# HGRN2 values for four heads in one matmul group, and the HGRN2 norm factor applied in the output stage

## The chip, the cores and the metric

One core of a Trainium2 chip runs the whole program. Five engines work side by side, each through its own instructions in order: TensorE (PE; its weight loads are the row PEld), VectorE (DVE), ScalarE (ACT), GpSimd (POOL) and SyncE (SP), which here mostly issues DMAs. The metric is the device time of one execution in microseconds (us), smaller is better. A change of 0.2% (3.8 us) is about what a measurement of this kernel can tell from no change.

## The reference, cut to what matters

A decoder layer on x of 2048 tokens by 1024 columns, in float32: h = RMSNorm(x), one input projection, two mixers side by side, one output projection, a residual and a last RMSNorm. The change concerns the HGRN2 mixer, eight heads of 128 keys and 128 values each:

```python
def hgrn2_mix(q_raw, f_raw, i_raw, g_raw, lb, norm_w):
    q = silu(q_raw); f = lb + (1 - lb) * sigmoid(f_raw); k = (1 - lb) * sigmoid(-f_raw)
    v = i_raw
    # per head, in chunks: S_t = diag(f_t) S_{t-1} + k_t v_t^T ;  o_t = S_t^T q_t
    ...
    o = o * lax.rsqrt(jnp.mean(o * o, axis=-1, keepdims=True) + EPS)   # over the 128 values
    o = o * norm_w
    o = o.reshape(B_, L, HG_WIDTH) * silu(g_raw)
    return o
```

The norm factor is one number for each token and head. The Mamba-2 mixer, which the change touches little, has such a factor for each token and group (two groups). Then `x = x + concat(hg_out, m2_out) @ w_out`.

## The kernel before

**Tiling.** Tokens go in 4 blocks of 512 (`TB`), each of 4 windows of 128 (`NW`). Activations lie as [channel, token]. Every operand of a projection is split into a high and a low part (`wh`, `wl` for weights, `hh`, `hl` for the normed input; `hr`, `lr` are those of block 0 before its norm factor is known), and a product is three matmul passes, wh·hh, wl·hh, wh·hl, over 8 slices of 128 input columns (`proj`, L345): 24 matmuls of 512 moving columns for 128 output columns. In block 0 the weights are split on ACT, DVE and POOL and saved to DRAM; blocks 1 to 3 read the two parts back.

**Units.** A block runs eight head units `H` (`hg_unit`, L608), eight Mamba units `M` (`m2_unit`, L476), two `B` units (`bc_unit`), one `dt_unit`, and the values `VV`. Each unit has projection steps (three of an `H`, two of an `M`) and later stages (`m0` to `m7` of a head), which are planned so many steps after the unit's start (`DUES`, L35) and run between the projection steps of later units (`plan`, `step`, `flush`, L828 to L839). `block_jobs` (L862) writes out the order of units. Each engine runs in that order, with small shifts by the scheduler.

**Values.** `v_step` (L582) makes v as [token, value] for a pair of heads: the stationary operand is a window of hh or hl, the moving operand 256 columns of weights, and two windows share a PSUM bank. There are two steps for a pair, four pairs a block.

**A head's end.** `m6` (L797) makes the result `po` as [token, value] (stationary att and qa, moving v and the states), squares it on ACT, sums on DVE (L808), makes the factor on POOL (L810) and multiplies on DVE (L812). `m7` (L816) transposes it back on PE (tile `oT`, four transposes), multiplies by the norm weight and the gate (L820) and stores it in DRAM (`mix_d`).

**Mamba norm.** The factors of a group are gathered in `rstg`, transposed and stored once for two blocks (`rg_store`, L853, tile `rgt`). The output stage reads them back broadcast to 128 partitions (`rgb`, L980) and multiplies (L985).

**Output stage.** For each block of tokens `mix_get` (L968) loads two of the 16 mixer tiles (`mr`), splits them into `mh` on ACT (L989) and `ml` on DVE or POOL (L990); `out_mm` (L994) runs three passes of matmuls into one PSUM bank for each of 8 output slices d. `wo_get` (L954) splits the output weights into `woh` on ACT (L959) and `wol` on DVE (L960). The first block starts early: for e = 0 to 8 (`NE` = 9) and the five d of `early` it runs between the last stages of block 3 (`early_step`, L1011); afterwards come e = 9 to 15 for those d, then all 16 e for the other three d, for which the mixes are loaded and split a second time. The tiles `mh`, `ml` share four buffers with the first two output weights, which stay, so two pairs are in flight.

**Memory.** Pools hold work tiles: slots of 512 (tag "s", 19), 1024 (tag "b", 7) and 768 elements; PSUM has 2 banks for projections (`pj`) and 6 for the rest (`px`). The pool `o1` of the output stage takes the place of `hh` and `hl`; a tile in it waits until the tile that lay there has been read for the last time.

## Time and profile before

| | us |
|---|---|
| median of 3 runs (1924.34 to 1927.28) | 1924.44 |
| the profiled execution | 1923.41 |
| its span | 1921.7 |
| PE busy in the span | 1886.1 (98%) |
| DVE busy | 1207.5 (63%) |
| ACT busy | 687.5 (36%) |
| POOL busy | 316.7 (16%) |
| mean granted TensorE clock, share of full speed | 0.996 |

The profiled execution took 1.7 us more than its span and 1.0 us less than the median. Busy shares are over the whole span. A matmul's listed duration reaches past the start of the next one, since they are pipelined, so what a matmul costs in a stream is the distance from its start to the next start. Rows in brackets name a group further below.

### The profile page before, as it was taken

The page shows a single profiled execution, that of the slowest core. Times are in us where ns is not written, and L with a number is a line of the kernel's source. Part 1 is how long each engine was busy: PE and PEld are TensorE (multiplying, and loading weights), DVE is VectorE, ACT ScalarE, POOL GpSimd, SP SyncE. Part 2 cuts the span into 40 slices and gives each one's busy share as a digit, 9 for nine tenths or more (in the row PEclk, how much of TensorE's full clock was granted, in tenths as well). Part 3 has the DMA queues.
Part 4 walks back from the last instruction along what each step waited for, and adds up shares of the span by engine and source line. Part 5 has one row for each costly group of instructions (what it writes and reads, how often), then busy time and mean ns, then how long its engine had stood idle before and what let it go on. Part 6 is the DMA issues. An engine that isn't in the chain of part 4 may idle for free. (4 is left out here: it accounts for less than half of the span.)

```text
span 1921.7 us, 35105 instructions
## 1 busy us (share of the span) xinstructions
PE 1886.1 (98%) x14056; PEld 1599.3 (83%) x14056; DVE 1207.5 (63%) x2904; ACT 687.5 (36%) x1156; POOL 316.7 (16%) x445
## 2 busy tenths in 40 slices
PE   7999999999999999999999999999999999999998
PEld 5788888788888888888888888888888877888898
DVE  8777788865666576655665866556655675424342
ACT  4554454433433343233333333323332433121211
POOL 4312242312011221110112211101110120000000
PEclk9999999999999999999999999999999999999999
DMA  8767777745555566355555554645554454414032
GB/s 266 253 229 262 260 258 250 252 171 175 175 187 189 184 198 192 128 187 174 178 199 176 206 168 137 194 165 167 171 171 164 152 192 170 159 50 148 28 111 88
DMA packets 110899, 344.97 MB, mean 180 GB/s; under 512 B 12224, under 2 KB 21008, under 8 KB 110352
## 3 DMA queue, kind: packets, MB, share of 16 engines
q1 hardware_dynamic: 109536, 341.46, 52.7%
q8 instruction: 111, 1.82, 0.4%
q0 software_dynamic: 96, 0.03, 0.4%
q10 hardware_dynamic: 1104, 1.24, 0.2%
q14 instruction: 52, 0.43, 0.1%
HBM read 262.82 MB, written 79.86 MB: 178 GB/s over the span
## 5 line engine op out<-in xcount | busy, mean ns | idle before, releaser
L999 PE MATMUL po<-mh,woh 128*128 128x512 f32 (+1 forms) x640 | 223.1, 352 | 2.1 <-ACT woh L959 2.1
L999 PE MATMUL po<-mh,wol 128*128 128x512 f32 (+1 forms) x640 | 222.6, 348 | 0.0
L999 PE MATMUL po<-ml,woh 128*128 128x512 f32 (+1 forms) x640 | 221.6, 348 | 0.0
L999 PEld LDWEIGHTS po<-mh,woh 128*128 128x128 f32 x640 | 121.4, 190 | 19.3 <-ACT woh L959 2.9
L999 PEld LDWEIGHTS po<-mh,wol 128*128 128x128 f32 x640 | 121.5, 190 | 16.0 <-issue 0.7
L999 PEld LDWEIGHTS po<-ml,woh 128*128 128x128 f32 x640 | 121.2, 190 | 15.1
L989 ACT CAST mh<-mr 128x1024 fp32r<-128x1024 f32 (+1 forms) x48 | 43.4, 907 | 190.1 <-PE po L999 156.5
L990 DVE TENSOR_TENSOR ml<-mr,mh 128x1024 fp32r<-128x1024 f32 (+1 forms) x46 | 47.5, 1032 | 88.7 <-ACT mh L989 88.4
L122 POOL TENSOR_SCALAR hr<-hss 128x4 f32<-128x4 f32 x32 | 8.3, 259 | 514.5 <-DVE hss L808 514.4
L511 DVE TENSOR_SCALAR csb<-csb,cs 128x128 f32<-128x128 f32 x256 | 66.8, 328 | 31.9 <-ACT ecs L508 31.9
L440 DVE SCALAR_TENSOR_TENSOR xs<-u_x,sm,xs 128x512 f32<-128x512 f32 x96 | 71.8, 748 | 4.2 <-ACT xs L438 3.6
L596 PE MATMUL pv<-wh,hh 128*128 128x256 f32 x480 | 70.2, 289 | 0.0
L596 PE MATMUL pv<-wl,hh 128*128 128x256 f32 x480 | 69.0, 285 | 0.0
L109 POOL TENSOR_TENSOR wl<-wr,wh 128x1024 fp32r<-128x1024 f32 x22 | 55.4, 2523 | 78.5 <-ACT wh L108 63.6
L353 PE MATMUL px<-hh,wh 128*128 128x512 f32 x256 | 67.6, 406 | 0.0
L353 PE MATMUL pz<-hh,wh 128*128 128x512 f32 x256 | 67.5, 405 | 0.0
L596 PE MATMUL pv<-wh,hl 128*128 128x256 f32 x480 | 67.3, 283 | 0.0
L353 PE MATMUL pf<-hh,wh 128*128 128x512 f32 x248 | 65.8, 405 | 0.0
L353 PE MATMUL pq<-hh,wh 128*128 128x512 f32 x248 | 65.2, 405 | 0.0
L353 PE MATMUL pg<-hh,wh 128*128 128x512 f32 x248 | 65.0, 404 | 0.0
L442 POOL TENSOR_TENSOR xs<-xs,u_x 128x512 f32<-128x512 f32 x32 | 41.9, 1310 | 133.8 <-ACT u_x L441 133.8
L353 PE MATMUL pz<-hh,wl 128*128 128x512 f32 x256 | 63.5, 390 | 0.0
(334 smaller groups left out, 4522.9 us busy)
## 6 DMA issues: line engine op xcount, KB each, us to landing
wh<-whd SPq DMA_DIRECT2D x156, 512.0 KB, 4.4
wl<-wld SPq DMA_DIRECT2D x156, 512.0 KB, 3.4
whd<-wh SPq DMA_DIRECT2D x52, 512.0 KB, 5.2
wld<-wl SPq DMA_DIRECT2D x52, 512.0 KB, 4.1
wr<-wt SPq DMA_DIRECT2D x51, 512.0 KB, 5.4
csb<-csd SPq DMA_DIRECT2D x32, 512.0 KB, 5.8
mr<-mixd SPq DMA_DIRECT2D x64, 256.0 KB, 2.9
mixd<-sg SPq DMA_DIRECT2D x32, 256.0 KB, 3.7
```

The lines of the kernel that those rows point to most:

```text
L109: (G if i in (1, 2) or c >= 32 else V).tensor_tensor(lo[:, z], raw[:, z], hi[:, z].bitcast(F32), op=ALU.subtract)
L122: G.tensor_scalar(r, ss, 1.0 / n, EPS, ALU.mult, ALU.add)
L353: state["mm"] = T.matmul(ps, lhsT=a[:, k, :], rhs=b[:, k, :], start=(n == 0), stop=(n == 23))
L440: V.scalar_tensor_tensor(dst, u[:, j:j + TB], cw[:, c, j:j + 1], dst, op0=ALU.mult, op1=ALU.add)
L442: G.tensor_tensor(dst, dst, u[:, 3:], op=ALU.mult)
L511: V.tensor_scalar(csb[:, i, w, :], csb[:, i, w, :], dts["cs"][:, w, h0 + i:h0 + i + 1], 0.0, ALU.subtract, ALU.min)
L596: T.matmul(ps[:, 256 * j:256 * j + 256], lhsT=a[:, k, w * P:(w + 1) * P], rhs=rhs, start=(n == 0), stop=(n == 23))
L989: A.copy(mh[:, :, 0:n], mr[:, :, 0:n])
L990: lo.tensor_tensor(ml[:, :, 0:n], mr[:, :, 0:n], mh[:, :, 0:n].bitcast(F32), op=ALU.subtract)
L999: T.matmul(pss[d], lhsT=a[:, d, :], rhs=b, start=(e == 0 and n == 0), stop=(e == 15 and n == 2))
```

## The change

Three things change together.

1. `v_step` makes the values of four heads at once. The moving operand is 512 weight columns. One step now takes a quarter of the input columns (two slices of 128) for all four windows, whose sums stay open in four PSUM banks (two of `pj`, two of `px`) over four steps. There are two groups of four steps a block instead of four groups of two, so `block_jobs` has the first group at the block's start and the second after M(3). The host lays out the weights to fit.
2. `m6` swaps the operands: stationary v and states, moving att and qa. The result comes out as [value, token], so the transposes go, and the gate and norm weight are applied straight from PSUM. The sum of squares now runs across partitions: `m7` is four matmuls with `ones` (tile `hss`, by `ss_cols`), a copy and the POOL pair, into a tile `nst` that holds the factors of all ten norms of a block.
3. `rg_store` runs in every block and stores 40 rows. In the output stage, `mix_get` reads for each head (e below 8) the broadcast factor (`rgb`, three buffers in `o1`, tile `rgh`) and multiplies `mr` by it on DVE before the split; for the last two half blocks the Mamba factors are read for each half.

Sizes follow: 17 slots "s" and 8 "b", `NE` = 8.

```diff
-    def v_step(tb, pr, i, ws, rec):
+    def v_step(tb, q, j, ws, rec):
...
-            for j in range(2):
-                w = 2 * i + j
+            if j == 0:
+                pjt = lambda w: pj.tile([P, TB], F32, tag="pj", name=f"pv{q}_{tb}_{w}")
+                pxt = lambda w: bank(f"pv{q}_{tb}_{w}")
+                rec["ps"] = [pjt(0), pxt(1), pxt(2), pjt(3)]
+                rec[tb] = [slot("b", [2, 4, P], f"v{q}{z}_{tb}") for z in range(2)]
+            for w in range(NW):
+                ps = rec["ps"][w]
                 n = 0
                 for a, b in ((hh, 0), (hh, 1), (hl, 0)):
-                    for k in range(KT):
-                        rhs = wv[k // 4][b].rearrange("p k c -> p (k c)")[:, (k % 4) * 256:(k % 4) * 256 + 256]
-                        T.matmul(ps[:, 256 * j:256 * j + 256], lhsT=a[:, k, w * P:(w + 1) * P], rhs=rhs,
-                                 start=(n == 0), stop=(n == 23))
+                    for k in range(2):
+                        rhs = wv[b].rearrange("p k c -> p (k c)")[:, k * TB:(k + 1) * TB]
+                        T.matmul(ps, lhsT=a[:, 2 * j + k, w * P:(w + 1) * P], rhs=rhs,
+                                 start=(j == 0 and n == 0), stop=(j == 3 and n == 5))
...
-                T.matmul(po[:, sl], lhsT=att[:, w, :], rhs=v[:, w, :], start=True, stop=False)
-                T.matmul(po[:, sl], lhsT=qa[:, sl], rhs=prevs[w], start=False, stop=True)
-            on = slot("s", [TB], f"on{nm}")
+                T.matmul(po[:, sl], lhsT=v[w], rhs=att[:, w, :], start=True, stop=False)
+                T.matmul(po[:, sl], lhsT=prevs[w], rhs=qa[:, sl], start=False, stop=True)
+            r["on"] = on = slot("s", [TB], f"on{nm}")
+            A.activation(on, po, AF.Square)
+            sg = r["sg"]
+            V.scalar_tensor_tensor(sg, po, hgn[:, hd:hd + 1], sg, op0=ALU.mult, op1=ALU.mult)
+            nc.sync.dma_start(mix_d[hd][tb], sg)
+            advance(hgS[:, hd, :], NW - 1)
+
+        def m7():
+            ssv = ss_cols(r["on"], bank(f"hss{nm}"))
             ss = mp.tile([P, NW], F32, tag="hss", bufs=2, name=f"hss{nm}")
-            A.activation(on, po, AF.Square)
-            V.tensor_reduce(ss, on.rearrange("p (w e) -> p w e", w=NW), axis=AX.X, op=ALU.add)
-            rr = mp.tile([P, NW], F32, tag="hr", bufs=2, name=f"hr{nm}")
-            rstd_cols(rr, ss, P)
...
-        def m7():
-            sg = r["sg"]
-            poT = bank(f"oT{nm}")
-            transpose4(poT, r["on"])
-            V.scalar_tensor_tensor(sg, poT, hgn[:, hd:hd + 1], sg, op0=ALU.mult, op1=ALU.mult)
-            nc.sync.dma_start(mix_d[hd][tb], sg)
+            V.tensor_copy(ss, ssv)
+            rstd_cols(nst[:, hd, :], ss, P)
...
+        if e < 8:
+            for i in range(2):
+                rgb = o1.tile([P, NW, P], F32, tag="rgb", bufs=3, name=f"rgh{bl}_{e}_{i}")[:, 0:n // P]
+                r0 = (e + i) * NW + c0 // P
+                nc.sync.dma_start(rgb, rg_d[tb][r0:r0 + n // P, :].partition_broadcast(P))
+                V.tensor_tensor(mr[:, i, 0:n], mr[:, i, 0:n], rgb.rearrange("p w t -> p (w t)"), op=ALU.mult)
...
-    NE = 9
+    NE = 8
```

PE at the opening of `VV(1)` in block 0: `pv` are the PSUM tiles of values, `wh`, `wl` the weight parts, `hh`, `hl` the stationary windows. Before:

```order
L596 MATMUL pv_0_0_1438<-wh_1253,hh_475 128x256 x4
L596 MATMUL pv_0_0_1438<-wh_1327,hh_475 128x256 x4
L596 MATMUL pv_0_0_1438<-wl_1254,hh_475 128x256 x4
L596 MATMUL pv_0_0_1438<-wl_1328,hh_475 128x256 x4
L596 MATMUL pv_0_0_1438<-wh_1253,hl_476 128x256 x4
L596 MATMUL pv_0_0_1438<-wh_1327,hl_476 128x256 x4
```

And now:

```order
L597 MATMUL pv_0_0_2283<-wh_2066,hh_479 128x512 x2
L597 MATMUL pv_0_0_2283<-wl_2067,hh_479 128x512 x2
L597 MATMUL pv_0_0_2283<-wh_2066,hl_480 128x512 x2
L597 MATMUL pv_0_1_2284<-wh_2066,hh_479 128x512 x2
L597 MATMUL pv_0_1_2284<-wl_2067,hh_479 128x512 x2
L597 MATMUL pv_0_1_2284<-wh_2066,hl_480 128x512 x2
```

One window of two heads was 24 matmuls of 256 columns; now six of 512 columns serve one window and four heads, then the next bank's turn comes. In the whole program 1536 matmuls become 768.

PE at the last stage of a head in block 0, between projection steps (`pf`, `pq`). Before:

```order
L353 MATMUL pf_0_1092<-hh_475,wh_961 128x512 x8
L353 MATMUL pf_0_1092<-hh_475,wl_962 128x512 x8
L353 MATMUL pf_0_1092<-hl_476,wh_961 128x512 x8
L359 MATMUL oT_0_1121<-ident,on_0_1067 128x128 x4
L353 MATMUL pq_0_1137<-hh_475,wh_1022 128x512 x8
```

And now, with the next stage matmul `H` behind it:

```order
L352 MATMUL pf_0_1868<-hh_479,wh_1654 128x512 x8
L352 MATMUL pf_0_1868<-hh_479,wl_1655 128x512 x8
L352 MATMUL pf_0_1868<-hl_480,wh_1654 128x512 x8
L129 MATMUL hss_0_1897<-ones,on_0_1805 128x2 x4
L738 MATMUL H_0_1906<-qa_0_1842,k_0_1443 32x32 x8
```

Four transposes have become four float32 matmuls with two moving columns each.

DVE where block 3 hands over to the output stage: where the first `ml` and `wol` stand, which the first output matmuls read. `MB`, `atq`, `tot`, `k` belong to head 7's early stages. Before:

```order
L990 TENSOR_TENSOR ml_0_16187<-mr_0_16183,mh_0_16186 128x1024
L680 TENSOR_TENSOR MB_7_3_15970<-MB_7_3_15970,tot_7_3_15973 128x64x2
L691 TENSOR_TENSOR MB_7_3_16068<-MB_7_3_15970,tot_7_3_15973 128x16x4x2
L681 TENSOR_TENSOR MB_7_3_15970<-MB_7_3_15970,tot_7_3_15973 128x64x4
L637 TENSOR_TENSOR sg_3_15942<-pg_3_15917,sg_3_15942 128x512
L667 TENSOR_TENSOR k_3_15796<-k_3_15796,f_3_15795 128x256
L669 TENSOR_TENSOR atq_3_15975<-A_3_15953,md_187 128x128
L693 TENSOR_TENSOR MB_7_3_16068<-MB_7_3_15970,tot_7_3_15973 128x16x4x4
L670 COPY_PREDICATED atq_3_15975<-md_187,A_3_15953 128x64
L703 TENSOR_TENSOR tot_7_3_15973<-tot_7_3_15973 128x64
L960 TENSOR_TENSOR wol_16193<-wor_16190,woh_16192 128x1024
```

And now:

```order
L708 TENSOR_TENSOR k_3_14971<-k_3_14971,tot_7_3_15258 128x16x24
L562 TENSOR_TENSOR y_3_15231<-y_3_15231,sz_3_14905 128x512
L715 COPY_PREDICATED atq_3_15159<-mask_202,B_7_3_15321 128x4x24
L976 TENSOR_TENSOR mr_0_15363<-mr_0_15363,rgh_0_0_15366 128x512
L715 COPY_PREDICATED atq_3_15159<-mask_202,B_7_3_15321 128x4x8
L976 TENSOR_TENSOR mr_0_15363<-mr_0_15363,rgh_0_1_15369 128x512
L715 COPY_PREDICATED atq_3_15159<-mask_202,B_7_3_15321 128x4x16
L510 TENSOR_SCALAR csb_3_15163<-csb_3_15163,cs_12093 128x128 x6
L989 TENSOR_TENSOR ml_0_15373<-mr_0_15363,mh_0_15372 128x1024
L953 TENSOR_TENSOR wol_15379<-wor_15376,woh_15378 128x1024
```

The first `ml` stood among head 7's first stages, some four steps ahead of its use. It now stands after the two new products, behind head 7's second level (`k`, L708, of the small form) and Mamba unit 7's first six `csb` rows, and the first `wol` behind it.

## Rows read from the trace of the kernel before

**Rows 1.** Page, part 1: engine, busy us, share of the span, instructions.

```profile
PE 1886.1 (98%) x14056; PEld 1599.3 (83%) x14056; DVE 1207.5 (63%) x2904; ACT 687.5 (36%) x1156; POOL 316.7 (16%) x445
```

**Rows 2.** PE's waits, three of 16 (first, sixth, last): total us, times, longest.

```profile
PE pf L353 <- ACT wh L108: 6.9, 1, 6.9
...
PE po L999 <- ACT woh L959: 2.1, 2, 1.8
...
PE hb L149 <- DVE dg_hr L148: 0.2, 1, 0.2
```

**Rows 3.** PE timeline, block 0: start, us, line, tile, instructions merged [wait].

```profile
122.79 1.12 PE L596 MATMUL pv<-wl,hh 128*128 128x256 f32 x8
123.75 1.12 PE L596 MATMUL pv<-wh,hl 128*128 128x256 f32 x8
...
137.50 1.98 PE L353 MATMUL pf<-hh,wl 128*128 128x512 f32 x8
139.32 1.98 PE L353 MATMUL pf<-hl,wh 128*128 128x512 f32 x8
141.13 0.60 PE L359 MATMUL kT<-ident,k 128*128 128x128 f32 x4
```

**Rows 4.** PE timeline, block 0: four transposes, and a sum with ones.

```profile
164.36 0.60 PE L359 MATMUL oT<-ident,on 128*128 128x128 f32 x4
164.89 0.55 PE L644 MATMUL B<-MB,k 128*32 128x48 f32 x32
...
257.05 0.95 PE L129 MATMUL mss<-ones,sqa 128*128 128x2 f32 x8
257.92 0.55 PE L644 MATMUL B<-MB,k 128*32 128x48 f32 x32
```

**Rows 5.** DVE by line: count, busy us, mean ns, idle before and who ended it.

```profile
L985 DVE SCALAR_TENSOR_TENSOR mr<-mr,sm,rgb 128x512 f32<-128x512 f32 (+1 forms) x48 | 31.4, 689 | 34.0 <-DMA mr<-mixd 34.0
...
L812 DVE TENSOR_TENSOR on<-o,hr 128x512 f32<-128x512 f32 x32 | 22.1, 692 | 30.0 <-POOL hr L123 30.0
...
L808 DVE TENSOR_REDUCE hss<-on 128x4 f32<-128x512 f32 x32 | 21.8, 682 | 2.0 <-ACT on L807 1.0
```

**Rows 6.** PE timeline, start of block 0: two waits for DVE.

```profile
45.45 0.87 PE L644 MATMUL B<-MB,k 128*32 128x48 f32 x32 [2.65 <-DVE MB L681]
...
74.08 0.41 PE L414 MATMUL cs<-xd,triu 128*128 128x64 f32 x2 [2.25 <-DVE xd L407]
```

**Rows 7.** End of block 0: engines by stretch (PE, PEld, DVE, ACT, POOL), and PE.

```profile
340.00:360.00 20.00, 19.53 (x188) 16.05 (x187) 19.12 (x45) 6.37 (x10) 5.07 (x5) 1.00 0.70 245
...
367.20 0.33 PE L738 MATMUL H<-qa,k 128*32 128x32 f32 x16 [2.34 <-DVE k L708]
```

**Rows 8.** PE timeline at the hand-over to the output stage.

```profile
1528.86 1.98 PE L353 MATMUL pz<-hl,wh 128*128 128x512 f32 x8
...
1533.93 0.50 PE L999 MATMUL po<-mh,woh 128*128 128x512 f32 x1
...
1569.29 1.05 PE L129 MATMUL mss<-ones,sqa 128*128 128x2 f32 x8 [1.57 <-POOL sqa L570]
```

**Rows 9.** DVE timeline at the same place.

```profile
1532.44 1.22 DVE L990 TENSOR_TENSOR ml<-mr,mh 128x1024 fp32r<-128x1024 f32 x1
...
1537.03 0.69 DVE L812 TENSOR_TENSOR on<-o,hr 128x512 f32<-128x512 f32 x1 [1.19 <-POOL hr L123]
...
1538.77 0.55 DVE L708 TENSOR_TENSOR k<-k,tot 128x384 f32<-128x384 f32 x1
```

**Rows 10.** ACT by line; and DMA issues: count, KB, us to landing.

```profile
L959 ACT CAST woh<-wor 128x1024 fp32r<-128x1024 f32 x16 | 16.5, 1048 | 16.5 <-DMA wor<-wout 14.8 <-issue 1.6
...
rgb<-rgd SPq DMA_DIRECT2D x10, 256.0 KB, 4.0
```

**Rows 11.** PE by stretch (busy, granted clock); ACT timeline, after block 3's last stages.

```profile
1572.00:1574.00 2.00, 2.00 (x6) 0.50 0.03 10
...
1578.17 2.95 ACT L959 CAST woh<-wor 128x1024 fp32r<-128x1024 f32 x3 [1.63 <-issue]
```

More of the change, by code (lines that the diff above doesn't have):

```diff
@@ L213, in hybrid_layer @@
     mix_d = [[dp.tile([P, TB], F32, name=f"mixd{e}_{t}") for t in range(NTB)] for e in range(16)]
-    rg_d = [dp.tile([32, P], F32, name=f"rgd{t}") for t in range(2)]
+    NR = (HG + 2) * NW
+    rg_d = [dp.tile([NR, P], F32, name=f"rgd{t}") for t in range(NTB)]
     cs_d = [dp.tile([NW * M2H, P], F32, name=f"csd{t}") for t in range(NTB)]
@@ L598, in p0 @@
                         n += 1
-            dst = rec[tb].rearrange("p w h e -> p w (h e)")
-            if tb in raw_rs:
-                for j in range(2):
-                    w = 2 * i + j
-                    A.activation(dst[:, w, :], ps[:, 256 * j:256 * j + 256], AF.Copy, scale=rsx[:, tb, w:w + 1])
-            else:
-                A.copy(dst[:, 2 * i:2 * i + 2, :].rearrange("p w c -> p (w c)"), ps)
+                if j == 3:
+                    dst = rec[tb][w // 2][:, w % 2].rearrange("p h e -> p (h e)")
+                    if tb in raw_rs:
+                        A.activation(dst, ps, AF.Copy, scale=rsx[:, tb, w:w + 1])
+                    else:
+                        A.copy(dst, ps)
@@ L780, in m5 @@
             kn = r["kn"]
-            v = vrec[tb][:, :, hd % 2, :]
+            v = [vrec[tb][w // 2][:, w % 2, hd % 4, :] for w in range(NW)]
             pS = bank(f"hS{nm}")
@@ L784, in m5 @@
                 sl = slice(w * P, (w + 1) * P)
-                T.matmul(pS[:, sl], lhsT=kn[:, sl], rhs=v[:, w, :], start=True, stop=True)
+                T.matmul(pS[:, sl], lhsT=kn[:, sl], rhs=v[w], start=True, stop=True)
             r["pS"] = pS
@@ L798, in m6 @@
             qa, att, prevs = r["qa"], r["att"], r["prevs"]
-            v = vrec[tb][:, :, hd % 2, :]
+            v = [vrec[tb][w // 2][:, w % 2, hd % 4, :] for w in range(NW)]
             po = bank(f"o{nm}")
@@ L851, in need, with rg_store @@
         return len(worder) - 1
-    def rg_store(half):
+    def rg_store(tb, nst):
         def m0():
-            pt = bank(f"rgt{half}")
-            T.transpose(pt[0:32, 0:P], rstg.rearrange("p a g w -> p (a g w)"), ident)
-            rgs = mp.tile([32, P], F32, tag="cst", bufs=1, name=f"rgs{half}")
-            A.copy(rgs, pt[0:32, 0:P])
-            nc.sync.dma_start(rg_d[half], rgs)
+            pt = bank(f"rgt{tb}")
+            T.transpose(pt[0:NR, 0:P], nst.rearrange("p a w -> p (a w)"), ident)
+            rgs = mp.tile([NR, P], F32, tag="cst", bufs=1, name=f"rgs{tb}")
+            A.copy(rgs, pt[0:NR, 0:P])
+            nc.sync.dma_start(rg_d[tb], rgs)
         return [], [(8, m0)]
@@ L865, in block_jobs, with VV @@
         dts, vrec, bcs, sq = {}, {}, {}, {}
+        nst = mp.tile([P, HG + 2, NW], F32, tag="nst", bufs=2, name=f"nst{tb}")
         add = lambda fn, *args: out_.append((fn, args))
         def H(hd):
-            add(hg_unit, tb, hd, [need(tb, c) for c in (8 + hd, hd, 24 + hd)], vrec.setdefault(hd // 2, {}), {})
-        def VV(pr):
-            ws = [need(tb, 16 + 2 * pr + i) for i in range(2)]
-            for i in range(2):
-                add(v_step, tb, pr, i, ws, vrec.setdefault(pr, {}))
+            add(hg_unit, tb, hd, [need(tb, c) for c in (8 + hd, hd, 24 + hd)], vrec.setdefault(hd // 4, {}), nst, {})
+        def VV(q):
+            ws = [need(tb, 16 + 4 * q + j) for j in range(4)]
+            for j in range(4):
+                add(v_step, tb, q, j, ws, vrec.setdefault(q, {}))
         def B(g):
@@ L916, in block_jobs @@
         call(nxt[0])
[L917 removed]
+        H(6)
         call(nxt[1])
[L919 removed]
+        M(6)
         call(nxt[2])
[L921 removed]
+        H(7)
         call(nxt[3])
[L923 removed]
         M(7)
[L925 to L926 removed]
+        add(rg_store, tb, nst)
         return out_
```

59 lines of the change are left out of this document (22 added, 37 removed).

## The prediction

> **What bounds the kernel now.** I read the page's first part before anything else: PE is busy 98% of the span, DVE 63%, ACT 36%, POOL 16% [rows 1]. So PE is the bound on average, and the question for any edit is whether it shortens PE's stream or moves one of PE's waits. The second view is the list of PE's waits: 16 lines, from 6.9 us down to 0.2, which add up to 28.6 us [rows 2]. Any gain beyond PE's own work has to come out of these 28.6 us. About half of them have no tie to the change (the first weights, the norm of x).
>
> Then I looked at three places in time. At the start of block 0 PE waits 2.65 and 2.25 us for DVE [rows 6]. At the end of block 0 DVE is busy 19.12 of 20 us while PE is busy 19.53, and 7 us after that stretch PE waits 2.34 us for DVE's `k` [rows 7]: there two engines are the bound together. At the hand-over PE ends the last projection pass (it starts at 1528.86) and starts its first output matmul at 1533.93 with no wait of note [rows 8]; the waits come later (1.57 us at 1569.29, and 2.1 us in two waits for `woh`) [rows 2, 8]. Blocks 1 to 3 hold no wait of PE that matters, so there PE's stream is the time.
>
> **PE's stream, part by part.** *Values.* The reader should look at starts, not durations: eight matmuls of 256 columns take 122.79 to 123.75, 0.96 us; eight of 512 take 1.82 us [rows 3]. That is 0.120 and 0.227 us each, so two short ones cost 0.240 where one long one costs 0.227: some 13 ns go with each matmul saved. Before there are 1536, 192 groups of eight: 192 x 0.96 = 184.3 us. After there are 768, 96 groups of eight: 96 x 1.815 = 174.2. **-10.1 us.** The columns moved are the same.
>
> *Sum across partitions.* Four transposes last from 164.36 to 164.89, 0.53 us; the sum with `ones`, which Mamba's norm already uses and a head now uses too, lasts 257.05 to 257.92, 0.87 us [rows 4]. A head loses the first and gains the second, +0.34, with 32 heads **+10.9 us**. The swapped operands of the result are 128 columns either way: 0. Two more transposes of factors (`rgt`): a single one is about a fourth of the 0.53, so 0.3 to 0.5 with its surroundings, +0.5. **PE's stream in sum: -10.1 + 10.9 + 0.5 = +1.3 us.** The two large terms nearly cancel: what the change wins in the values it spends on a reduction that the transposed layout forces on PE.
>
> Beside the row on the values stands a rule of the Trainium skill ("TensorE: Matmul & The Clock Gate", section "Back-to-back issue gap"): an isolated matmul's gap is N/2.4 + 2.5 ns at the full clock. By that a saved matmul is worth 2.5 ns, 768 of them an estimated 1.9 us, and the sum would be 8.2 us higher. The row here has 13 ns, so the measurement speaks against the rule, and I go by the row.
>
> **DVE and POOL in the blocks.** A head loses on DVE the sum (682 ns), the multiplication (692) and the idle time ahead of it, 30.0 us for 32 heads, 0.94 each [rows 5]; it gains a copy of four columns. That is 2.3 us of DVE's time a head. In blocks 1 to 3 PE does not wait for DVE, so the saving is worth 0 there: PE's own stream covers it.
>
> *Start of block 0.* There it can pay. `VV(0)` is now four steps instead of two, so PE has some 11 us of values (two more steps of 24 x 0.227) to do while DVE catches up, and both waits of [rows 6] stand behind it. The bounds: at best both vanish and a little more, -6; at worst the two more weight tiles that are split in that time, on the engines that are waited for, delay something else, +1 (about a cast of 1.05 us [rows 10]). I take the `cs` wait shrunk and the `B` wait mostly kept, because the first projection still waits for weights: **-1.5**.
>
> *End of block 0.* The old order had value steps, which ask nothing of DVE, between the last head units. Now they are done after M(3), and H(6), M(6), H(7), M(7) follow each other with the preparation of block 1 in between. DVE had 0.9 us of slack in 20 [rows 7]. For it: two or three heads end there, 2.3 us of DVE each. Against it: a value step of 10.9 us (48 x 0.227) that served as cover is gone. Bounds: -4 (the 2.34 us wait and its neighbours go) to +10 (the cover goes and nothing replaces it). I take **+1**, near the middle, because the saved 5 to 7 us answer about half to two thirds of the lost cover and the present waits may shift rather than grow.
>
> **The hand-over, the main term.** Here the change adds a chain ahead of the first output matmul. Before, `ml` ended at 1533.66 (1532.44 + 1.22) [rows 9], `mh` and the first `woh` earlier still. Now a broadcast factor must be loaded, `mr` multiplied by it twice, and only then can `mh` and `ml` be made.
>
> *When the factor can arrive.* Its buffer is in `o1`, on the memory of block 3's `hh`, and is free when the last pass that reads `hh` ends, 1528.86 [rows 8]. A broadcast of 256 KB lands 4.0 us after its issue [rows 10]: 1532.9 at the earliest.
>
> *When DVE can multiply.* The products (0.69 us each [rows 5]) stand behind head 7's `k` of L708, which before ran at 1538.77 for 0.55 us [rows 9], to 1539.3. Of what stood ahead of it the change takes away `ml` (1.22), one head's sum (0.68) and the multiplication with its wait (0.69 + 1.19, [rows 9]): 3.8 us less, but `y` of a Mamba unit now stands ahead, and small copies; with those I estimate +1.0. So about 1536.5; two products, 1537.9 to 1538.2 with the two small copies between.
>
> *What follows.* ACT makes `mh`; a tile of that size takes 1.05 us there [rows 10]: 1539.1. The first `woh` now stands behind `mh` on ACT: another 1.05, 1540.1. PE, ready at 1533.93, waits **6.2 us**. The first `wol` stands behind six `csb` rows and `ml` on DVE, and the three matmuls that need only `mh` and `woh` cover 0.7 us: **+1.2** more. Behind the waiting products on DVE are head 7's remaining copies and `csb`; PE waits for those too, but not beyond the same stall. Behind the load on SP's queue are the next factors, the next `mr` and two stores of mixes, all needed later.
>
> *Clock.* After PE's 1.57 us wait the granted clock is 0.50 for at least 2 us (1.2 GHz instead of 2.4) [rows 8, 11], so at least 1.0 us is lost. A wait four times as long costs the same kind; I take **+1.7**.
>
> *e = 8.* It no longer runs early, so at 1575 PE comes to it right after the transposed factors: copy, then the casts of `woh` (2.95 us for three, with 1.63 of idle issue ahead [rows 11]) and `wol`. Between 2.4 and 4: **+3.2**.
>
> From this go the old waits that the new ones take the place of: 2.1 for `woh`, 1.57 for `sqa` (POOL catches up during the long stall), and the clock's 1.7 behind it, 5.4. Net 6.2 + 1.2 + 1.7 + 3.2 - 5.4 = **+6.9**, with bounds 0 (DVE is ready when the load lands: the stall is then 1532.9 + 1.4 + 2.1 - 1533.9 = 2.5, and e = 8 costs nothing) and +12 (nothing old goes).
>
> **After that.** The mixes of the first half block are loaded a second time for the other three d. Two pairs are in flight, and 18 matmuls of a pair and three d take 18 x 0.227 = 4.1 us, so a pair has 8.2 us for its loop: factors 4.0, products 1.4, `mh` 1.05, `ml` 1.1, in sum 7.6 plus issue. Three factor buffers serve pairs that need two each, in SP's order. Tight: **+1.5** (0 to 4). Later pairs have eight d, 10.9 us: hidden. The new products add some 22 us to DVE, which in the output stage has that much idle; the tail is unchanged.
>
> **Sum**, on the profiled execution of 1923.4 us: +1.3 - 1.5 + 1.0 + 6.9 + 1.5 = +9.2, so 1932.6. The median shown is 1.0 us above that execution: **1934 us** as a measured median. With its own bounds, taking half of each since they won't all fall one way, this case runs from about 1927 to 1942.
>
> **Rivals.**
> A, faster: DVE's relief reaches PE. Both waits of [rows 6] and the one of [rows 7] vanish (-7.2), and at the hand-over DVE is so far ahead that the load alone decides (stall 2.5 instead of 6.2, the old waits gone, -1.5). 1923.4 + 1.3 - 7.2 - 1.5 + 1.0 = **1917**. It decides if DVE reaches the first product before 1533. Against it: 3.8 us less work ahead of the product, where 6 are needed, and a DVE that is full in [rows 7].
> B, no change: the stall at the hand-over is only half the size, and start and end of block 0 give 3 us. **1925**. For it: the scheduler's shifts around the hand-over are worth 2 or 3 us each way.
> C, slower still: DVE becomes the bound in the long stretches of heads without values, at the end of each block and not of block 0 alone. With DVE 96% busy in [rows 7] and 10.9 us of cover gone, 3 to 5 us a block: 1934 + 15 = **1949**. It decides if DVE's share in blocks 1 to 3 there is above 95%; 63% over the span speaks against it, as does 2.3 us less a head.
> D, the values are not faster: four open banks in turn, six matmuls on each, keep the pitch of a 512 group at twice 0.120 us, and -10.1 becomes 0: **1944**. Against it: projections of 512 columns run at 0.227 with the same rows. By the skill's rule above it would be near this.
>
> **How the numbers follow.** Forecast 0.57, B 0.17, C 0.10, A 0.09, D 0.07. The range 1922 to 1946 leaves out A, most of C and thin tails, together 0.2. About 0.2% (3.8 us) is what a measurement of this kernel can tell from no change, so "same" is 1920.6 to 1928.3. Faster: A and a tail of B, 0.10. Same: most of B and the low end of the forecast, 0.20. Slower: the rest, 0.70.
>
> **What the new profile would show.** Values: starts of 512 groups of eight 1.82 us apart and 768 of them; if 1.92, D. `hss`: 0.87 us; if 0.53, +10.9 goes and the kernel is clearly faster. At the hand-over, PE's waits on `po` for `woh` or `mh` of 5 to 7 us, then `wol`, and a granted clock near 0.5; if the first product on DVE starts by 1533 (relative to the last `pz` pass: 4 us after it), A or B. At the start, the `cs` wait smaller than 2.25. In block 0's end, waits on DVE of 3 to 6 us in sum; much more there, or waits of over 1 us in blocks 1 to 3, is C. I would be most wrong if the order at the hand-over hides the chain behind other work, or if the end of block 0 runs dry.

## The result

| kernel | median, us | against the kernel before |
|---|---|---|
| before (same set of runs) | 1924.39 | |
| changed | 1938.53 (1935.05 to 1939.89) | 1.0068, 95% interval 1.0051 to 1.0086 |

The change makes the kernel 14.1 us slower. 1934 us had been forecast, with 1922 to 1946 as the range. The direction and the place of the loss were right; its size was two thirds of what came.

### The profile after

First the page's part 1 (engine, busy us, share, instructions), beside [rows 1]. PE is still busy 98% of the span, now 9 us longer:

```profile
PE 1895.2 (98%) x13418; PEld 1577.9 (81%) x13418; DVE 1203.2 (62%) x2920; ACT 710.3 (37%) x1170; POOL 323.2 (17%) x444
```

Next PE's waits (total us, times, longest), beside [rows 2]:

```profile
PE po L998 <- ACT woh L952: 9.7, 2, 6.0
...
PE B L644 <- DVE MB L681: 3.9, 1, 3.9
...
PE po L998 <- DVE ml L989: 2.0, 2, 1.7
...
PE H L738 <- DVE k L708: 1.7, 1, 1.7
...
PE po L998 <- DVE wol L953: 1.5, 2, 1.0
```

The new first line holds most of the loss: two waits, 9.7 us in sum, for output weights, where the kernel before had 2.1.

To see where in the program the time goes, I cut it at one mark: the first `pz` pass of the last Mamba unit of each block. Rows of PE's timeline (start, us, line, tile), the kernel before, blocks 0 to 3:

```profile
390.90 2.11 PE L353 MATMUL pz<-hh,wh 128*128 128x512 f32 x8
769.50 2.11 PE L353 MATMUL pz<-hh,wh 128*128 128x512 f32 x8
1148.32 2.11 PE L353 MATMUL pz<-hh,wh 128*128 128x512 f32 x8
1525.09 2.11 PE L353 MATMUL pz<-hh,wh 128*128 128x512 f32 x8
...
1913.58 1.22 PE L149 MATMUL po<-dg_fz,ones 128*128 128x256 f32 x2 [1.89 <-DVE dg_fz L148]
```

and the changed kernel:

```profile
391.95 2.12 PE L352 MATMUL pz<-hh,wh 128*128 128x512 f32 x8
770.49 2.12 PE L352 MATMUL pz<-hh,wh 128*128 128x512 f32 x8
1149.01 2.12 PE L352 MATMUL pz<-hh,wh 128*128 128x512 f32 x8
1525.74 2.12 PE L352 MATMUL pz<-hh,wh 128*128 128x512 f32 x8
...
1928.94 1.22 PE L149 MATMUL po<-dg_fz,ones 128*128 128x256 f32 x2 [1.89 <-DVE dg_fz L148]
```

The last row of each is PE's last matmul. Subtracting neighbours gives five pieces. The same was done for every kernel below, with the same two kinds of rows:

| piece, us | before | changed | changed again | values alone | result alone | product ahead | ahead and nine weights | PE kept busy | float32r sum | all three | log and exp |
|---|---|---|---|---|---|---|---|---|---|---|---|
| start to mark 0 | 390.9 | 392.0 | 394.4 | 395.0 | 391.1 | 392.0 | 396.9 | 396.0 | 393.0 | 394.2 | 385.3 |
| mark 0 to 1 | 378.6 | 378.5 | 378.5 | 376.1 | 381.0 | 378.5 | 378.5 | 378.5 | 374.9 | 374.9 | 373.6 |
| mark 1 to 2 | 378.8 | 378.5 | 378.5 | 376.2 | 381.0 | 378.5 | 378.5 | 378.5 | 374.9 | 374.9 | 373.7 |
| mark 2 to 3 | 376.8 | 376.7 | 376.7 | 373.5 | 379.1 | 376.8 | 376.8 | 376.7 | 373.1 | 373.1 | 371.9 |
| mark 3 to the last matmul | 388.5 | 403.2 | 404.8 | 390.5 | 400.7 | 395.1 | 393.2 | 401.2 | 398.1 | 393.6 | 386.7 |

The middle three pieces repeat to a tenth of a microsecond in kernels with the same blocks, so they can be read like a scale. The first piece can't: five executions that have the same block 0 (changed, changed again, product ahead, ahead and nine weights, PE kept busy) took 392.0 to 396.9. The changed kernel gains up to 0.3 us in each of the blocks 1 to 3 and loses 14.7 us behind the last mark.

What moves in the first and the last piece can be read in the window view (PE, PEld, DVE, ACT, POOL busy; the granted clock follows them). The start of block 0 in the changed kernel, then in the one with the product ahead and nine weights:

```profile
20.00:50.00 30.00, 26.91 (x170) 20.96 (x171) 26.61 (x52) 10.46 (x16) 10.60 (x7) 0.94 0.79 285
```

```profile
20.00:50.00 30.00, 27.05 (x160) 21.05 (x160) 24.47 (x49) 9.19 (x15) 9.81 (x6) 0.83 0.73 247
```

And 50 to 70, around and behind the wait for `MB`, before, then changed:

```profile
50.00:70.00 20.00, 19.66 (x152) 14.65 (x151) 18.26 (x43) 9.88 (x19) 10.00 (x11) 1.00 0.71 253
```

```profile
50.00:70.00 20.00, 16.10 (x110) 12.02 (x109) 11.34 (x24) 8.39 (x16) 8.74 (x8) 0.83 0.58 211
```

PE's busy time in windows of 1 us, times the part of the clock that was not granted there, gives an estimate of what the low clock cost; a window's length less PE's busy time is what PE stood idle (in the last column 5.4 us of the busy time make nothing that is used, see further below):

| us | before | changed | changed again | product ahead | ahead and nine weights | PE kept busy |
|---|---|---|---|---|---|---|
| first piece: idle | 21.1 | 19.9 | 22.0 | 20.2 | 21.3 | 21.5 |
| first piece: low clock (estimate) | 1.6 | 6.1 | 7.1 | 6.0 | 10.5 | 9.5 |
| last piece: idle | 6.3 | 15.1 | 14.9 | 9.9 | 8.7 | 8.6 |
| last piece: low clock (estimate) | 1.9 | 6.6 | 8.8 | 3.4 | 3.1 | 6.2 |

So the first piece varies by 5 us between executions mostly because the granted clock does: less idle and low clock, it is 365.0 to 366.0 us in all five of the same block 0. The last piece of the changed kernel is 14.7 us longer than before by 8.8 us of idle time, 4.7 of low clock and 1.2 of the rest.

PE's timeline there, at the hand-over, beside [rows 8]:

```profile
1534.10 0.55 PE L644 MATMUL B<-MB,k 128*32 128x48 f32 x32
1540.70 1.65 PE L998 MATMUL po<-mh,woh 128*128 128x512 f32 x3 [6.05 <-ACT woh L952]
1543.33 0.79 PE L998 MATMUL po<-mh,wol 128*128 128x512 f32 x1 [0.98 <-DVE wol L953]
1543.92 0.63 PE L998 MATMUL po<-ml,woh 128*128 128x512 f32 x1
1544.35 0.63 PE L998 MATMUL po<-mh,wol 128*128 128x512 f32 x1
...
1548.19 0.63 PE L998 MATMUL po<-ml,woh 128*128 128x512 f32 x1
1548.61 0.99 PE L129 MATMUL hss<-ones,on 128*128 128x2 f32 x8
```

DVE at the same place, beside [rows 9] (the two `mr` rows are the new products):

```profile
1536.00 0.55 DVE L708 TENSOR_TENSOR k<-k,tot 128x384 f32<-128x384 f32 x1
...
1537.24 0.68 DVE L976 TENSOR_TENSOR mr<-mr,rgh 128x512 f32<-128x512 f32 x1
...
1537.94 0.68 DVE L976 TENSOR_TENSOR mr<-mr,rgh 128x512 f32<-128x512 f32 x1
```

and ACT:

```profile
1538.66 1.04 ACT L988 CAST mh<-mr 128x1024 fp32r<-128x1024 f32 x1 [0.84 <-DMA mr<-mixd]
1539.61 1.99 ACT L952 CAST woh<-wor 128x1024 fp32r<-128x1024 f32 x2
```

Read them as one chain: the second product ends at 1538.6, `mh` starts at 1538.66 (the 0.84 us ahead of it is put down to a DMA that had long landed; it was the product), the cast of `woh` behind it, and PE starts at 1540.70. The factor's load did not hold the product: DVE shows no idle time ahead of it, only its own queue. Then look at the distances of PE's starts: 0.43 us from 1543.92 to 1548.61, where [rows 3] have 0.227. PE runs at half pace for some 5 us after its stall. The window view says so too, beside [rows 11]:

```profile
1540.00:1545.00 5.00, 3.32 (x7) 2.21 (x8) 4.80 (x10) 2.65 (x3) 2.10 (x3) 0.50 0.70 231
1545.00:1550.00 5.00, 5.00 (x34) 4.07 (x34) 3.26 (x6) 1.11 (x2) 0.03 (x1) 0.63 0.85 296
```

The same happens a second time at e = 8, with durations of 0.63 us up to 1592.49:

```profile
1582.88 0.27 PE L851 MATMUL rgt<-ident,nst 128*40 128x128 f32 x1
1586.80 1.22 PE L998 MATMUL po<-mh,woh 128*128 128x512 f32 x2 [3.64 <-ACT woh L952]
...
1592.49 0.63 PE L998 MATMUL po<-mh,woh 128*128 128x512 f32 x1
```

### The profile page after: what moved, and what is told of

It reads as the page before. It is cut to its first block, busy times and chain, and to the rows that moved or that the text cites. A ratio compares the mean times of both kernels' runs of the same rounds, so it can differ in the third digit from the quotient of the medians.

```text
span 1937.3 us, 34016 instructions
## 1 busy us (share of the span) xinstructions
PE 1895.2 (98%) x13418; PEld 1577.9 (81%) x13418; DVE 1203.2 (62%) x2920; ACT 710.3 (37%) x1170; POOL 323.2 (17%) x444
## 3 DMA queue, kind: packets, MB, share of 16 engines
q8 instruction: 106, 1.74, 0.4%
## 4 chain that ended last, share of the span: by engine, by line
PE 90%; DVE 5%; DMA 3%; ACT 1%; issue 1%; POOL 0%; ACTq 0%; DVEq 0%; SPq 0%; POOLq 0%
PE po L998 15%; PE px L352 9%; PE pz L352 9%; PE pf L352 9%; PE pv L597 9%; PE pq L352 9%; PE pg L352 8%; PE pB L352 2%; PE pC L352 2%; PE yd L546 2%; PE B L644 1%; PE o L804 1%; PE S L537 1%; PE hS L785 1%; PE o L803 1%; PE yo L557 1%
## 5 line engine op out<-in xcount | busy, mean ns | idle before, releaser
L794 DVE SCALAR_TENSOR_TENSOR hSt<-hgS,totw,hS 128x128 f32<-128x128 f32 x32 | 11.0, 345 | 111.9 <-PE hS L785 99.2
L597 PE MATMUL pv<-wh,hh 128*128 128x512 f32 x224 | 72.0, 402 | 0.0
L569 POOL TENSOR_TENSOR sqa<-sqa,ecs 128x512 f32<-128x512 f32 x24 | 32.0, 1332 | 228.4 <-ACT ecs L568 191.9
L597 PE MATMUL pv<-wl,hh 128*128 128x512 f32 x224 | 69.5, 391 | 0.0
L597 PE MATMUL pv<-wh,hl 128*128 128x512 f32 x224 | 69.1, 390 | 0.0
L708 DVE TENSOR_TENSOR k<-k,tot 128x384 f32<-128x384 f32 x64 | 43.7, 683 | 40.8 <-PE B L644 40.8
L434 ACT COPY u_x<-px 128x512 f32<-128x512 f32 x32 | 18.8, 586 | 129.4 <-PE px L352 129.4
```

Source lines behind the costliest of these rows:

```text
L569: G.tensor_tensor(sq["acc"], sq["acc"], t, op=ALU.add)
L597: T.matmul(ps, lhsT=a[:, 2 * j + k, w * P:(w + 1) * P], rhs=rhs, start=(j == 0 and n == 0), stop=(j == 3 and n == 5))
L708: V.tensor_tensor(kv, kv, tt[:, :, 1:4].unsqueeze(3).broadcast_to([P, ng, 3, b]), op=ALU.mult)
```

## The experiments

Four questions were open: do the values pay and the sums cost what the rows said; is the chain through the factor what stalls PE; is the low clock a cost of its own that follows from the stall; and can the reduction be had for less. The runs came in three sets on one chip each, so that a run is compared through its ratio to the kernel before of its own set (1923.8, 1925.0 and 1924.0 us).

### The two halves of the change

*Values alone*, on the kernel before:

```diff
-                        T.matmul(ps[:, 256 * j:256 * j + 256], lhsT=a[:, k, w * P:(w + 1) * P], rhs=rhs, ...)
+                        T.matmul(ps, lhsT=a[:, 2 * j + k, w * P:(w + 1) * P], rhs=rhs, ...)
```

with the order of units, slots and weight layout of the change.

> The kernel before with the first part of the change alone: values of four heads at once, the new order of units, the new numbers of slots; a head's end and the output stage as before. Theory (the working of the prediction): PE's stream loses 10.1 us, the start and the end of block 0 together change by -1.5 to +2, the hand-over stays as it was: 1914 to 1917 us. Rival D (a saved matmul saves nothing): 1924 or more. Rival C (the stretches without value steps leave DVE as the bound, more so here, since DVE keeps its sums and multiplications): 1925 to 1935, with waits of PE for DVE in every block.

Measured: 1919.91 us, 0.9976 (0.9964 to 0.9989): -3.9 us, above the expected 1914 to 1917. In the blocks the forecast holds: -2.5, -2.6 and -3.3 us from mark to mark, -2.5 expected. Over the first of them that is 2.51 us for 192 matmuls saved, 13 ns each, as [rows 3] had it. The Trainium skill's 2.5 ns for an isolated matmul ("TensorE: Matmul & The Clock Gate", "Back-to-back issue gap") is not what this stream shows. Rival D is out (in the changed kernel two of the new matmuls take 0.46 us, from 47.46 to 47.92, where four of the old took 0.48), and rival C too, since blocks 1 to 3 hold no wait above 0.6 us. Behind the last mark it loses 2.0 us (the `sqa` wait of [rows 8] is 2.73 here, and the low clock behind it). Marks and last piece make -6.4 us; the median says -3.9; so block 0 costs some 2.5 us, which is what the total missed by. Its end shows how, where the values no longer cover DVE, which here still has its sums and products:

```profile
350.00:360.00 10.00, 9.03 (x97) 7.83 (x101) 9.96 (x23) 6.24 (x10) 3.81 (x4) 1.00 0.79 314
360.00:370.00 10.00, 6.81 (x60) 5.09 (x51) 9.16 (x20) 0.00 (x0) 3.12 (x3) 0.96 0.63 213
370.00:380.00 10.00, 10.00 (x55) 7.88 (x56) 8.97 (x18) 6.92 (x13) 6.35 (x7) 0.70 0.59 213
```

DVE is full, PE stands for over 3 us of 360 to 370, and the granted clock falls to 0.70 behind that.

*Result alone*: the changed kernel with `v_step`, the order of units and the slots of the kernel before.

```diff
-                T.matmul(po[:, sl], lhsT=v[w], rhs=att[:, w, :], start=True, stop=False)
+                T.matmul(po[:, sl], lhsT=v[:, w, :], rhs=att[:, w, :], start=True, stop=False)
```

> The changed kernel with the first part undone: values of two heads at once, old order of units and slots, but results as [value, token], sums across partitions on PE, and factors in the output stage. Theory: PE's stream +10.9 for the sums and +0.5 for the factors, and the hand-over and output stage +13 to +15 as the trace of the changed kernel shows them: 1948 to 1951 us. If the two parts add up, this result and that of the values alone, each against the kernel before, sum to the whole change (+14.1). Rival: the output stage's loss comes from the new order of units (head 7 and Mamba unit 7 crowd DVE at the end of block 3), then this stands at 1936 to 1940.

Measured: 1942.54 us, 1.0096 (1.0080 to 1.0112): +18.8, below the expected 1948 to 1951 and above the rival's 1936 to 1940. A block costs 2.2 to 2.4 us more, 0.28 to 0.30 for each of its eight heads, where 0.34 had been reckoned. The piece behind the last mark costs +12.2, with the same waits of 6.05 and 3.64 us for `woh`: the output stage loses its time without the new order of units, so this run's rival falls. Marks and last piece make +19.1, the median +18.8, so block 0 as a whole stays as it was. The two halves add up: -3.9 + 18.8 = +14.9 against +14.1 for the whole change.

### The chain at the hand-over

*Product ahead*: the changed kernel, the first pair loaded and multiplied ahead of the last Mamba unit.

```diff
+    def mix_ahead():
+        ahead["mr"] = mr = wp.tile([P, 2, TB], F32, tag="raw", bufs=3, name="mr0_0")
...
+            rgb = slot("s", [NW, P], f"rgh0_0_{i}")
+            nc.sync.dma_start(rgb, rg_d[0][i * NW:i * NW + NW, :].partition_broadcast(P))
+            V.tensor_tensor(mr[:, i, :], mr[:, i, :], rgb.rearrange("p w t -> p (w t)"), op=ALU.mult)
...
+        if tb == NTB - 1:
+            call(mix_ahead)
         M(7)
```

> The changed kernel; the first pair of mixes (heads 0 and 1 of block 0) with its two factors is loaded into work slots and multiplied two projection steps before the output stage, so that no product stands ahead of the first split any more. Theory (the chain load, product, split, cast makes the stall at the hand-over): PE's waits of 6.05 and 0.98 us there and the low clock behind them, some 3 us, go: -8 to -10, 1929 to 1931 us. Rival 1: the first split or the first woh is late for another reason (ACT behind head 7, a weight buffer), a stall of 3 us stays and the clock falls as before: 1933 to 1935. Rival 2: the time comes back at e = 8 to 10, where PE now arrives 10 us earlier at the transposed factors: 1936 to 1938.

In the trace the stall is gone. PE's timeline there:

```profile
1534.11 0.55 PE L644 MATMUL B<-MB,k 128*32 128x48 f32 x32
1534.58 0.50 PE L1017 MATMUL po<-mh,woh 128*128 128x512 f32 x1
1534.92 0.39 PE L1017 MATMUL po<-mh,wol 128*128 128x512 f32 x1
1535.15 0.39 PE L1017 MATMUL po<-ml,woh 128*128 128x512 f32 x1
...
1545.02 0.50 PE L1017 MATMUL po<-mh,woh 128*128 128x512 f32 x1 [0.99 <-ACT mh L1007]
```

PE goes straight on at 0.23 us a matmul; one wait of 0.99 us for the next pair is new. Behind the mark it took 395.1 us, 8.1 less than the changed kernel, inside the expected 8 to 10. The first piece of the two traces is alike (392.0 us, 6.1 and 6.0 of them low clock), and so are the blocks, so the two executions differ by this piece alone. The times don't show it: 1935.82 us median, above the expected 1929 to 1931, 1.0069 (1.0049 to 1.0089), no better than the changed kernel's 1.0068. They spread from 1930.94 to 1942.37, more than the first piece does, in two groups: three of 1930.94 to 1932.55 us at a mean granted clock of 0.992 to 0.993, three of 1939.10 to 1942.37 at 0.989. Over 1930 us 0.004 of the clock is an estimated 7.7 us. The profiled execution was the fastest of them; where the others lost their clock no trace shows. So the trace shows that the chain made the stall, and the times leave open how much of the 8.1 us a typical execution keeps.

*Ahead and nine weights*: also `NE` = 9, with the third factor buffer in another pool.

```diff
-    NE = 8
+    NE = 9
```

> As the run with the first product ahead, and nine output weights taken early again instead of eight (the third factor buffer lies in another pool for that, and the early steps have two). Theory: the wait of 3.64 us for woh at e = 8, that for wol of 0.53 and the low clock behind them (2 to 3 us) go, some 0.3 us stay: -5 to -6 against that run, 1923 to 1926 us. Rival: with two factor buffers the early pairs wait for their loads, or the wait moves to e = 9 in full: 0 against that run.

Measured: 1934.34 us, 1.0052 (1.0037 to 1.0068). The wait of 3.64 us at e = 8 went, as expected; 0.22 stands at e = 9 and 1.35 at e = 12. But the last piece fell by 1.9 us, not 5 to 6, and the time missed the expected 1923 to 1926. The answer is in the list of waits:

```profile
PE mss L129 <- POOL sqa L569: 4.2, 1, 4.2
```

Without the stalls PE comes earlier to Mamba's last sum of squares and waits there for POOL, with the low clock behind it. Of this wait the kernel before had 1.57 us [rows 8], the changed kernel none: PE got there at 1578.53, and POOL's `sqa` had ended at 1576.08.

### The clock

*PE kept busy*: the changed kernel, with matmuls whose result is thrown away in the place of the stall.

```diff
+        if e == 0:
+            for _ in range(6):
+                T.matmul(pss[0], lhsT=ones, rhs=hgS[:, 0:4, :].rearrange("p a b -> p (a b)"), start=True, stop=True)
         out_mm(0, e, early)
```

> The changed kernel; six float32 matmuls of 512 columns on constants and old states, whose result is thrown away, stand ahead of the first output matmul, so that PE works through most of its wait there; the chain of load, product, split and cast stays. Theory (the granted clock falls because PE stands idle): the wait shows 1 us or less instead of 6.05, the clock stays at 1.00 behind it, and the 3.5 us of slow matmuls between 1540 and 1550 go: -3 us, 1935 us. Rival: the clock falls anyway, or the slow matmuls cover waits for wol and the next pair that then appear in full: 0, 1938 to 1939.

```profile
1538.58 5.42 PE L1016 MATMUL po<-hgS,ones 128*128 128x512 f32 x12
1544.70 1.42 PE L998 MATMUL po<-mh,woh 128*128 128x512 f32 x5 [0.70 <-ACT woh L952]
...
1547.91 0.40 PE L998 MATMUL po<-mh,wol 128*128 128x512 f32 x1
1548.15 0.40 PE L998 MATMUL po<-ml,woh 128*128 128x512 f32 x1
```

```profile
1545.00:1550.00 5.00, 4.84 (x41) 4.01 (x39) 5.00 (x9) 2.47 (x6) 2.50 (x3) 1.00 0.75 228
```

The chain is as long as before, and PE starts its first output matmul as late (14.96 us behind the mark in both), but the granted clock stays at 1.00 and the matmuls are 0.24 us apart instead of 0.43. So the low clock at this place came from PE standing idle, not from the chain. From the arrival of the first `wol`, 17.59 us behind the mark in both, to the end of e = 0 PE needs 2.44 us instead of 6.47. Of these 4.0 us some 2.4 are the clock; the rest is work that this kernel does ahead of `wol` (five matmuls instead of three, and a sum). It does not keep all of it: PE now waits 1.97 us for `sqa`, with a low clock behind that, so the low clock of the whole last piece is 6.2 us, hardly less than the changed kernel's 6.6, and the piece is 2.0 to 3.6 us shorter.

The time is 1938.59 us against 1942.60 of the changed kernel in the same set, 1.0072 (1.0060 to 1.0084) against 1.0089. Within the set the work that computes nothing gained 4.0 us, 3 expected; the intervals overlap, and the first comparison's changed kernel had 1.0068, so the gain over the whole kernel is less sure than the clock.

*The changed kernel again*, as the partner of that set.

> The changed kernel itself, unchanged, as the partner of the other runs beside it. It was 14.1 us above the kernel before, 1.0068 [1.0051, 1.0086]; expected again: 1.006 to 1.009, 1936 to 1940 us. The times of the runs with the product ahead spread over 11 us (1931 to 1942) while their trace is 8 us shorter than that of the changed kernel; should this run come out at 1.004 or less, the gain of those runs was smaller than their trace says, and above 1.008 larger.

1942.60 us, 1.0089 (1.0076 to 1.0102): the ratio at the upper end of what was expected, the time 2.6 us above it, the last piece 1.6 us longer than in the first trace. That too is the clock: behind the second wait for `ml` (1.76 us here, 1.74 there) it fell to 0.50 here and stayed at 1.00 there. By the ratios (1.0089 or 1.0068 against 1.0069) the product ahead saved 3.8 us or nothing, by the last pieces 8.1 to 9.7; the runs do not settle it further. With the float32r sum the same two repairs give 5.4 us by the ratios (1.0004 to 0.9976, below) and 4.5 by the last pieces, which agree.

### The price of the sum

*float32r sum*: the changed kernel, with the squares and the ones in float32r.

```diff
-            A.activation(on, po, AF.Square)
+            A.activation(on.bitcast(F32R), po, AF.Square)
...
-            ssv = ss_cols(r["on"], bank(f"hss{nm}"))
+            ssv = ss_cols(r["on"].bitcast(F32R), bank(f"hss{nm}"), one=onesr)
```

> The changed kernel; the squares of a head and the column of ones are float32r instead of float32, so that the sum across partitions is four matmuls in one pass each instead of two. Theory (the sum costs what its passes over 128 columns of weights cost, eight of 0.11 us): 0.44 us less for each of 32 heads, -12 to -14 us, 1925 to 1927. Rival 1: what counts is the dependence on a reduction that PE waits for, not its passes; then a head keeps 0.88 us and the time is 1938. Rival 2: a float32r pass loads weights at the same pace but starts later behind other work: -5.

Measured: 1925.72 us, 1.0004 (0.9995 to 1.0012), 16.9 below the changed kernel in the same set, more than the 12 to 14 expected. PE's timeline, the changed kernel and this one, in block 1:

```profile
441.44 0.95 PE L129 MATMUL hss<-ones,on 128*128 128x2 f32 x8
442.25 2.11 PE L352 MATMUL pq<-hh,wh 128*128 128x512 f32 x8
```

```profile
442.02 0.50 PE L129 MATMUL hss<-onesr,on 128*128 128x2 f32 x4
442.38 2.09 PE L354 MATMUL pq<-hh,wh 128*128 128x512 f32 x8
```

Eight instructions in 0.81 us became four in 0.36. The time went with the weight loads: PEld has eight of them end to end there, from 441.22 to 442.22, and here four, from 441.79 to 442.35. Blocks are 3.6 us shorter, 0.45 a head. The stalls behind the last mark stay (9.7 us for `woh`), as they must, but the last piece is 5.1 to 6.7 us shorter, and the two sums in it are 0.9 of that: the waits for `ml` fell from 2.0 to 0.2 us, which had not been reckoned.

*All three repairs* together:

> The changed kernel with all three repairs: first product ahead, nine early output weights, and the sum across partitions in float32r. Theory (the three costs are separate): the run with the first two (1934.3, 1.0052) less what float32r gave (1942.6 to 1925.7, 16.9 us): 1916 to 1920 us, below the kernel before and near the values alone (0.9976). Rival: with shorter heads PE arrives earlier at POOL's sqa and at the first weights of the output stage, and half of the gain returns as waits: 1925.

1919.68 us, 0.9976 (0.9967 to 0.9985), as expected: by the ratios the gains add up to within 2 us, and what is left is as fast as the values alone. The last piece is not shorter than with the first two repairs (393.6 and 393.2 us); the float32r sum pays in the blocks. Its largest wait in the output stage is the one for `sqa`, 4.9 us.

### A version that beats both

The factor need not go to the output stage. If the ones are the stationary operand and the squares move, one matmul of 512 columns leaves every token's sum on all partitions, and the factor can be multiplied in the block. The first try put the power on POOL, on top of the values alone:

```diff
+            T.matmul(ps, lhsT=onesr, rhs=on.bitcast(F32R), start=True, stop=True)
+            rr = slot("s", [TB], f"hr{nm}")
+            A.activation(rr, ps, AF.Copy, scale=1.0 / P, bias=EPS)
+            G.tensor_tensor(rr, rr, mhalf.broadcast_to([P, TB]), op=ALU.pow)
+            V.tensor_tensor(sg, sg, rr, op=ALU.mult)
```

> The kernel with values alone (1919.9 us), with this end of a head: the result as [value, token] as in the change, its squares in float32r, one matmul of ones by 512 columns that leaves the sum on all partitions, scale and epsilon on ACT, the power on POOL over 512 columns, and the factor multiplied on DVE in the block; nothing of the norm in the output stage. Theory: PE has 0.23 instead of 0.53 us a head, -9.6; DVE loses the sum across a row and the wait for POOL, which shortens the end of block 0 by 2 to 3 us; the hand-over as before: 1906 to 1911 us. Rival: the power over 512 columns takes POOL 10 us or more a head, and POOL, in order, holds up att, sqa and the convolution: 1920 or more.

4455.65 us, 2.3139 (2.3112 to 2.3167). The rival was right by far. POOL by line:

```profile
L820 POOL TENSOR_TENSOR hr<-hr,mhalf 128x512 f32<-128x512 f32 x32 | 2629.0, 82155 | 38.9 <-ACT hr L819 31.5 <-issue 6.2 <-POOL att L731 0.9
```

A power over 512 columns takes 82.2 us. In the kernel before, over four columns, POOL's power is 1.01 us (line L123, 32 times), which had hidden the price of a column.

The second try takes the power off POOL:

```diff
-            A.activation(rr, ps, AF.Copy, scale=1.0 / P, bias=EPS)
-            G.tensor_tensor(rr, rr, mhalf.broadcast_to([P, TB]), op=ALU.pow)
+            A.activation(rr, ps, AF.Ln, scale=1.0 / P, bias=epst)
+            A.activation(rr, rr, AF.Exp, scale=-0.5)
```

> The head's end of the run that took 4456 us, with the power taken off POOL: after the one float32r matmul that leaves the sum on all partitions, ACT makes the logarithm and the exponential of -0.5 times it over 512 columns, and DVE multiplies in the block. Theory: PE 0.23 instead of 0.53 us a head (-9.6), the end of block 0 shorter by 2 to 3 us: 1905 to 1911 us, the lowest so far. Against it stand 89 more table loads on ACT of 1.28 us each, 3.6 us a head and more with the two operations, on an engine that is 36% busy. Rival: ACT is late for a stage that PE waits for at the end of block 0 and at the hand-over, and 5 to 10 us come back: 1915 to 1920.

1904.39 us, 0.9905 (0.9890 to 0.9920): the fastest of all, just under the expected 1905 to 1911 and 19.6 us below the kernel before. PE in block 1, and ACT's table loads by line:

```profile
434.28 0.39 PE L817 MATMUL hss<-on,onesr 128*128 128x512 f32 x1
434.51 1.99 PE L355 MATMUL pq<-hh,wh 128*128 128x512 f32 x8
```

```profile
L819 ACT ACT_TABLE_LOAD x32 | 41.1, 1283 | 0.6
L820 ACT ACT_TABLE_LOAD x32 | 41.1, 1283 | 0.6
```

The sum costs PE 0.23 us, a block is 4.9 to 5.1 us shorter than before, and the hand-over has no factor in it (386.7 us behind the mark). Its trace also has the least low clock of all those shown, by the same estimate 1.7 us in the first piece and none behind the last mark. ACT pays with a table load ahead of each of the 64 operations and 25 more elsewhere, but it is busy only 44% of the span, and apart from the first weights and the first normed input PE's waits for it in the blocks come to 0.3 us.

## Why the prediction was right, and where its size was off

**Values, -10.1 us.** Right: -2.5, -2.6, -3.3 us a block where they stand alone.

**Sum across partitions and factors, +11.4 us.** Right in kind, a little high: 2.2 to 2.4 us a block, 0.28 to 0.30 a head instead of 0.34. Together with the values, blocks 1 to 3 came out up to 0.3 us shorter each, where the sum of +1.3 us had meant 0.3 longer.

**Start of block 0, -1.5 us.** The `cs` wait of 2.25 us went, as reckoned. The `B` wait, taken to be mostly kept, grew from 2.65 to 3.9 us, and the one for `lr` from 2.02 to 3.44. PE's idle time in the first 75 us is the same as before (17.0 and 16.9 us), and the low clock there, which the prediction put at nothing, went from 1.6 to 4.4 us (4.0 to 7.1 in the five traces of the same block 0). So the start gave none of its 1.5 us by waits, and the clock took some 3 us more.

**End of block 0, +1 us.** The two forces named there show where the halves run apart. With the cover gone and DVE's work kept (values alone), block 0 costs some 2.5 us; with both changed, the marks and the last piece make 14.3 of the first comparison's 14.1 us and 15.9 of the second's 17.7, so block 0 costs -0.2 to +1.8. (The first pieces themselves say +1.1 to +6.0, beside the one trace of the kernel before.) In the changed kernel's trace the waits for `k` and `mvA` are 1.71 and 1.28 us, beside 2.34 and 1.37 before. Behind them the granted clock falls here too: 1.7 to 3.4 us of low clock from 340 us on, where the kernel before had none. That block 0 by the medians came out near the forecast is luck in part: its waits and its stream were better than reckoned, and its clock worse.

**Hand-over, +6.9 us.** The chain was right link by link. The product had been put at 1536.5, it ran at 1537.24; the stall at 6.2 us, it was 6.05; the wait for `wol` at 1.2, it was 0.98; e = 8 at 3.2, it was 3.64, and 0.53 for `wol` at e = 11. **The mis-sized term is the clock.** I took 1.7 us for one stall, the same as what goes. The two stalls cost it twice: at the first one, eleven matmuls from 1543.92 to 1548.61 took 4.7 us, 2.2 more than at the pace of [rows 3], and the four ahead of them some 1.3 more; behind the second one, the thirteen matmuls up to 1592.91 lose about 3 us. Some 6.4 us instead of 1.7. About 1.5 of these were spent ahead of a first `wol`, where a faster PE would have waited for DVE instead, so the clock's own price is nearer 5. I had reckoned that a wait "four times as long costs the same kind"; what was not reckoned is that e = 8 makes a second stall, with a clock loss of its own.

**After that, +1.5 us.** Two waits for `ml`, 1.74 and 0.23 us: 2.0.

Summed: waits behind the mark 13.2 us instead of 4.4 (+8.8), low clock 6.6 instead of 1.9 (+4.7), the rest +1.2, together the 14.7 of the table, where 8.4 had been forecast. Rival B (half the stall) fails at the stall of 6.05 us, and rivals C and D have no support in any run. Rival A, a faster kernel, failed at the condition that it named: DVE reached the first product at 1537.24, not before 1533. One sum of the prediction is off without consequence: half of each bound, as it says, makes 1925 to 1944 and not 1927 to 1942.

What stays open: why the granted clock falls behind the same wait in one execution and not in another, or for longer. It moves the first piece by 5 us and the last by 2, and no run here takes that apart.

## What to carry to other kernels

When a step is moved from a place with slack to the first thing that a new stage needs, write down the whole chain ahead of that stage's first matmul, and price the stall twice: its length, and PE's slow restart behind it. An operation that feeds two columns through a full stationary tile cost its weight loads here (0.81 us for eight, 0.36 for four), so ask how many passes its type makes, and whether the operands can be swapped so that the columns move. Halves of a change that meet on one engine should be run apart: here a gain of 3.9 us and a loss of 18.8 lay in one number.
